# Second product of the feed-forward block, eight products of quarters against seven (Strassen's scheme, one level)

## The chip, the cores and the metric

One core of one Trainium2 chip runs the whole program. The metric is device time in microseconds (us), as the median of three runs: 895.64 us (895.19 to 899.47). One further execution was recorded by the profiler. TensorE is called PE below, VectorE DVE, ScalarE ACT, GpSimd POOL; SP and ACT issue the transfers (DMAs).

## The reference

The kernel computes one transformer block for 512 tokens of width 1024: a mixer of three attention branches, an attention over a memory, and a gated feed-forward network, each added to the residual stream, and a last normalization. Only the feed-forward part and the end bear on the change:

```python
def _swiglu(u, w_in, w_out):
    a = u @ w_in
    return (jax.nn.silu(a[..., :D_FF]) * a[..., D_FF:]) @ w_out

h = h + _swiglu(_rmsnorm(h, norm_ffn[l]), w_ffn_in[l], w_ffn_out[l])
return _rmsnorm(h, norm_final)
```

`D_FF` is 2816, that is 22 chunks of 128. The second product, `(silu * gate) @ w_out`, multiplies a 512 x 2816 matrix A by the 2816 x 1024 matrix B = `w_ffn_out`.

## The kernel before, in words

Every large product is made of three matmuls in place of one, since each operand is held as two float32r parts: `hi`, the rounded value, and `lo`, what is left. `split` (L60 to L68) makes the parts: one cast for `hi` (ACT, L58) and one subtraction for `lo` (L66, on DVE, or on POOL where `lo_eng` says so). `mm3` issues hi*hi (L94), hi*lo (L95) and lo*hi (L96). A matmul has 128 rows of the contraction and up to 512 columns.

The instructions are written in program order, and a scheduler sets the order of each engine's queue from it when the program is built; each engine then works through its own queue in order, and semaphores carry the waits between them. A tile pool with `bufs=n` hands out n buffers under a name; a tile that takes a buffer over waits until every reader of the tile before it is done.

The feed-forward's first product (`ff_pair`, called for pairs of chunks) fills four PSUM banks, applies tanh and two DVE operations (L824, L825), and splits the result into `act_hi` and `act_lo` of one chunk. Its weights come through `load_split`: 512 KB by DMA into `raw` (three buffers), then `whi` and `wlo` (three each).

The second product then runs over the 22 chunks k. It holds the whole 512 x 1024 result in eight PSUM banks, `wo` and `y` (four blocks of 128 tokens by two halves of 512 columns), and for each chunk loads 128 rows of B, splits them and issues 8 x 3 matmuls of 512 columns:

```python
mm3(yb[c, half], [t[:, cc(c)] for t in act[k]], [t[:, 0, n] for t in ws[k]], k == 0, False)
```

The last five chunks (`tail`) are done block by block, so that the end of one block of tokens (residual addition L868, squares L869, the scale of the normalization in `rms_scale`, the product with the gain L875 to L878, and the store) lies beside the matmuls of the next.

## Time and profile before

| | |
|---|---|
| median of three runs | 895.64 us |
| the profiled execution's own time | 895.49 us |
| its span in the profile | 893.7 us |
| PE busy | 857.5 us, 96% of the span |
| DVE, ACT, POOL busy | 57%, 46%, 16% |
| granted PE clock, mean | 0.994 of full speed |

How to read it: the span is the time from the first to the last recorded instruction; the run's own time is 1.79 us longer. An engine's busy time is the union of its instructions. A matmul's duration in the timeline is longer than the step from one to the next, because matmuls overlap in the array; the step is what a stream of them costs. A row such as `[2.24 <-DVE rs]` gives the engine's idle time ahead of the instruction and whom it waited for.

### The profile page before, as it was taken

How to read it: one execution, taken by the hardware profiler on the slowest of the kernel's cores; microseconds unless marked ns; L12 is line 12 of the kernel's file. 1: busy time of each engine (PE TensorE's matmuls, PEld its weight loads, DVE VectorE, ACT ScalarE, POOL GpSimd, SP SyncE). 2: the span in 40 equal slices, each digit the busy share in tenths (PEclk: the TensorE clock that was granted, in tenths of full speed). 3: DMA queues.
4: the chain of work that ended last, by engine and by line, in shares of the span. 5: the costliest groups of instructions: out<-in, count | busy, mean ns of one | idle time of the engine just before them, and what ended most of it. 6: DMA issues, size and time to landing. Idle time of an engine off the chain costs nothing.

```text
span 893.7 us, 13079 instructions
## 1 busy us (share of the span) xinstructions
PE 857.5 (96%) x5012; PEld 732.9 (82%) x5012; DVE 506.3 (57%) x1155; ACT 411.3 (46%) x779; POOL 141.0 (16%) x116
## 2 busy tenths in 40 slices
...
GB/s 321 88 110 24 37 64 120 141 49 25 58 35 27 97 94 140 187 175 249 124 149 183 182 48 166 190 165 94 95 95 95 95 98 105 124 96 95 95 19 76
DMA packets 93710, 99.00 MB, mean 111 GB/s; under 512 B 4656, under 2 KB 81616, under 8 KB 93648
## 3 DMA queue, kind: packets, MB, share of 16 engines
...
## 4 chain that ended last, share of the span: by engine, by line
PE 86%; DVE 6%; ACT 4%; DMA 2%; issue 1%; POOL 0%; SPq 0%; DVEq 0%; ACTq 0%; POOLq 0%
PE wo L95 9%; PE wo L96 9%; PE wo L94 9%; PE gf L95 6%; PE gf L94 6%; PE gf L96 6%; PE ff L96 4%; PE ff L94 4%; PE ff L95 4%; PE gm L94 3%; PE gm L95 3%; PE gm L96 3%; PE y L96 2%; PE y L95 2%; PE y L94 2%; PE av L101 2%
## 5 line engine op out<-in xcount | busy, mean ns | idle before, releaser
L58 ACT CAST whi<-raw 128x1024 fp32r<-128x1024 f32 (+1 forms) x167 | 174.6, 1048 | 283.3 <-PE y L96 70.1
L66 DVE TENSOR_TENSOR wlo<-raw,whi 128x1024 fp32r<-128x1024 f32 (+1 forms) x131 | 164.0, 1255 | 202.1 <-ACT whi L58 201.8
L66 POOL TENSOR_TENSOR wlo<-raw,whi 128x1024 fp32r<-128x1024 f32 x36 | 89.1, 2479 | 311.1 <-ACT whi L58 266.6
L95 PE MATMUL wo<-ut_lo,whi 128*128 128x256 f32 (+1 forms) x320 | 105.8, 331 | 0.0
L96 PE MATMUL wo<-ut_hi,wlo 128*128 128x256 f32 (+1 forms) x320 | 105.0, 328 | 0.0
L94 PE MATMUL wo<-ut_hi,whi 128*128 128x256 f32 (+1 forms) x320 | 104.8, 328 | 0.0
L96 PE MATMUL gf<-ut_hi,wlo 128*128 128x512 f32 (+1 forms) x192 | 69.8, 363 | 0.0
L94 PE MATMUL gf<-ut_hi,whi 128*128 128x512 f32 (+1 forms) x192 | 69.3, 361 | 0.0
L95 PE MATMUL gf<-ut_lo,whi 128*128 128x512 f32 (+1 forms) x192 | 69.3, 361 | 0.0
L94 PE MATMUL ff<-ut_hi,whi 128*128 128x512 f32 (+1 forms) x192 | 67.9, 354 | 0.0
L95 PE MATMUL ff<-ut_lo,whi 128*128 128x512 f32 (+1 forms) x192 | 67.9, 354 | 0.0
L96 PE MATMUL ff<-ut_hi,wlo 128*128 128x512 f32 (+1 forms) x192 | 67.9, 354 | 0.0
L95 PEld LDWEIGHTS wo<-ut_lo,whi 128*128 128x128 f32 x320 | 61.4, 192 | 6.3 <-issue 1.0
L94 PEld LDWEIGHTS wo<-ut_hi,whi 128*128 128x128 f32 x320 | 61.2, 191 | 5.7 <-issue 0.7
L96 PEld LDWEIGHTS wo<-ut_hi,wlo 128*128 128x128 f32 x320 | 61.3, 192 | 5.6 <-issue 0.4
L876 POOL TENSOR_TENSOR ut_hi<-ut_hi,ut_lo 128x512 f32<-128x512 f32 x4 | 5.1, 1293 | 361.9 <-ACT ut_hi L875 361.9
L94 PE MATMUL gm<-whi,ut_hi 128*128 128x256 f32 (+1 forms) x160 | 47.5, 297 | 0.0
L95 PE MATMUL gm<-wlo,ut_hi 128*128 128x256 f32 (+1 forms) x160 | 46.7, 292 | 0.0
L96 PE MATMUL gm<-whi,ut_lo 128*128 128x256 f32 (+1 forms) x160 | 46.5, 291 | 0.0
L96 PEld LDWEIGHTS gf<-ut_hi,wlo 128*128 128x128 f32 x192 | 36.2, 188 | 5.7 <-issue 1.2
L94 PEld LDWEIGHTS gf<-ut_hi,whi 128*128 128x128 f32 x192 | 36.2, 188 | 5.3 <-issue 0.8
L95 PEld LDWEIGHTS gf<-ut_lo,whi 128*128 128x128 f32 x192 | 36.2, 188 | 5.3 <-issue 0.8
...
## 6 DMA issues: line engine op xcount, KB each, us to landing
raw<-in_w_ffn_in_dram SPq DMA_DIRECT2D x56, 512.0 KB, 3.6
raw<-in_w_in_dram SPq DMA_DIRECT2D x46, 512.0 KB, 3.8
raw<-in_w_ffn_out_dram SPq DMA_DIRECT2D x22, 512.0 KB, 3.5
raw<-in_w_out_dram SPq DMA_DIRECT2D x16, 512.0 KB, 3.6
raw<-in_w_up_dram SPq DMA_DIRECT2D x8, 512.0 KB, 4.0
xt<-in_x_dram SPq DMA_DIRECT2D x4, 512.0 KB, 9.3
raw<-in_w_mem_kv_dram SPq DMA_DIRECT2D x4, 512.0 KB, 3.9
raw<-in_w_mem_q_dram SPq DMA_DIRECT2D x4, 512.0 KB, 3.9
```

Of the source, the lines that this page charges most:

```text
L58: nc.scalar.copy(dst, src)
L66: (lo_eng or nc.vector).tensor_sub(dst_lo, src, dst_hi.bitcast(F32))
L94: nc.tensor.matmul(dst, lh, rh, start=first, stop=False, skip_group_check=True)
L95: nc.tensor.matmul(dst, lh, rl, start=False, stop=False, skip_group_check=True)
L96: return nc.tensor.matmul(dst, ll, rh, start=False, stop=last, skip_group_check=True).ins
L101: nc.tensor.matmul(dst[64 * x:64 * x + 64], lhs[x], rhs[x], start=first, stop=last, skip_group_check=True)
L876: nc.gpsimd.tensor_mul(yo[:, n], yo[:, n], gain[:, n])
```

## The change

A and B are cut into quarters: A11 and A21 are the first and the last 256 tokens of chunks 0 to 10, A12 and A22 those of chunks 11 to 21; B11, B12 (chunks 0 to 10) and B21, B22 (chunks 11 to 21) are the left and right 512 columns. Seven products of quarters take the place of eight. They are those of Winograd's form of the scheme, with S1 = A21+A22, S2 = S1-A11, S3 = A11-A21, S4 = A12-S2, T1 = B12-B11, T2 = B22-T1, T3 = B22-B12, and B21-T2.

- `ff_pair` no longer splits its result. It keeps it in plain float32 (`sa` tiles for A11 and A21, `sb` tiles for A12 and A22), and `combine` forms S1, S2 and S4 on DVE and S3 on POOL, 128 x 256 each, once per chunk pair (k, k+11).
- First loop, k from 0 to 10, called a **turn** below: two DMAs bring 128 rows of B each; three DVE subtractions of 128 x 512 write T1, T3 and T2 into one tile `ts`, of which there is one buffer; ACT casts `ts` (128 x 1536), POOL subtracts for its `lo` part (128 x 1536); B11 is split on ACT and DVE; A11, S3 (one 128 x 512 piece) and S1, S2 (another) are split on ACT and DVE into `ahi` and `alo` (two buffers each); DVE writes B21-T2 over the A11/S3 tile. From turn 1 on the weights' parts lie in the buffers of the first product's input (`big`, the tiles `ut_hi` and `ut_lo`), turn k in half k%2. PE then does four products, 24 matmuls of 512 columns: A11*B11 into banks X, S2*T2 into Y, S1*T1 into Z, S3*T3 into V.
- Between the loops, ACT copies X into `u2`, DVE adds Y to it, and Z and V are added to the residual rows; six additions of 128 x 512 on POOL spread `u2` (L921 to L923).
- Then three passes of 66 matmuls each add a product into banks X, Z and V: A12*B21, S4*B22, A22*(B21-T2). A pass goes by pairs of chunks (`operands`), five pairs and one single; the `lo` part of the weights is made by DVE and POOL in turn. The second halves of `w_ffn_out` are loaded again, 12 more DMAs of 512 or 256 KB. The store of the first 256 tokens lies in the third pass, and the last three chunks of that pass are done block by block.

```diff
@@ after.py, lines 806 to 843 @@
+    def combine(k):
+        a11, a21 = (qta[k][:, x, :] for x in range(2))
+        a12, a22, s1, s2, s4 = (qtb[k][:, x, :] for x in range(5))
+        nc.vector.tensor_add(s1, a21, a22)
+        nc.vector.tensor_sub(s2, s1, a11)
+        nc.gpsimd.tensor_sub(a21, a11, a21)
+        nc.vector.tensor_sub(s4, a12, s2)
...
-            hi, lo = act[2 * fp + f]
-            split(hi[:, cols], lo[:, cols], s)
+            dst = (qtb if x else qta)[k][:, 0:2, :].rearrange("p a n -> p (a n)")
+            nc.vector.scalar_tensor_tensor(dst[:, cols], s, 0.5, b, op0=ALU.mult, op1=ALU.mult)
+            if x and cols.stop == S:
+                combine(k)
@@ after.py, lines 869 to 923 @@
+    def rows_split(src, lo_eng=nc.vector):
+        t = [f1.tile([P, 1024], F32R, name=n, bufs=2) for n in ("ahi", "alo")]
+        for (d0, n), ap in src:
+            split(t[0][:, d0:d0 + n], t[1][:, d0:d0 + n], ap, lo_eng=lo_eng)
+        return t
+    def product(banks, ka, kb, first, last):
+        for c in range(2):
+            mm3(banks[c], [t[:, cc(c)] for t in ka], kb, first, last)
+    for k in range(NH):
+        raw = []
+        for kk in (k, k + NH):
+            r = stage.tile([P, WT], F32, name="raw", bufs=3)
+            nc.sync.dma_start(r, wf[:, kk, :])
+            raw.append(r)
+        b11, b12 = raw[0][:, 0:512], raw[0][:, 512:1024]
+        b21, b22 = raw[1][:, 0:512], raw[1][:, 512:1024]
+        ts = f1.tile([P, 3, 512], F32, name="ts")
+        t1, t3, t2 = (ts[:, x, :] for x in range(3))
+        nc.vector.tensor_sub(t1, b12, b11)
+        nc.vector.tensor_sub(t3, b22, b12)
+        nc.vector.tensor_sub(t2, b22, t1)
...
+            wh, wl = (t[:, k % 2] for t in big)
+            w = [(wh[:, x, :], wl[:, x, :]) for x in range(4)]
+            split(wh[:, 1:4, :], wl[:, 1:4, :], ts, lo_eng=nc.gpsimd)
+        split(w[0][0], w[0][1], b11)
+        flat = qta[k].rearrange("p a n -> p (a n)")
+        a = rows_split([((0, 512), flat), ((512, 512), qtb[k][:, 2:4, :].rearrange("p a n -> p (a n)"))])
+        nc.vector.tensor_sub(flat, b21, t2)
+        for banks, x, y in ((X, 0, 0), (Y, 3, 3), (Z, 2, 1), (V, 1, 2)):
+            product(banks, [t[:, 256 * x:256 * x + 256] for t in a], w[y], k == 0, k == NH - 1)
...
+    for c in range(2):
+        nc.gpsimd.tensor_add(h[c][:, d1], u2[:, c, :], h[c][:, d1])
+        nc.gpsimd.tensor_add(h[2 + c][:, d0], u2[:, c, :], h[2 + c][:, d0])
+        nc.gpsimd.tensor_add(h[2 + c][:, d1], u2[:, c, :], h[2 + c][:, d1])
@@ after.py, lines 930 to 981 @@
+    def operands(k0, x, src):
+        ks = range(k0, min(k0 + 2, NH))
+        lo_eng = (nc.vector, nc.gpsimd)[k0 // 2 % 2]
...
+            hl = load_split((len(ks), 512), [wf[:, NH + k0:NH + k0 + len(ks), src]], lo_eng)
+            w = [[t[:, i, :] for t in hl] for i in range(len(ks))]
+        a = rows_split([((256 * i, 256), qtb[k][:, x, :]) for i, k in enumerate(ks)])
...
+    for banks, x, src, rows, n in ((X, 0, d0, 0, d0), (Z, 4, d1, 0, d1)):
+        for k0 in range(0, NH, 2):
+            for a, w, k in operands(k0, x, src):
+                product(banks, a, w, False, k == NH - 1)
+        for c in range(2):
+            nc.vector.tensor_add(h[rows + c][:, n], banks[c], h[rows + c][:, n])
+    for c in range(2):
+        store(c)
+    held = []
+    for k0 in range(0, NH, 2):
+        ops = operands(k0, 1, None)
...
+    for c in range(2):
+        for a, w, k in held:
+            mm3(V[c], [t[:, cc(c)] for t in a], w, False, k == NH - 1)
+        nc.vector.tensor_add(h[2 + c][:, d0], V[c], h[2 + c][:, d0])
+        store(2 + c)
```

What this makes of the queues, at three places. First, DVE at the start of the second product before, where each of 22 chunks has one subtraction (`wlo`); the rows ahead of it end the first product:

```order
L825 SCALAR_TENSOR_TENSOR sa_7946<-sa_7946,ff_7824 128x512 [waits DVE_49,PE_49]
L66 TENSOR_TENSOR act_lo20_7819<-sa_7946,act_hi20_7818 128x512 [waits Activation_49]
L825 SCALAR_TENSOR_TENSOR sa_7952<-sa_7952,ff_7825 128x512 [waits PE_49]
L66 TENSOR_TENSOR act_lo21_7821<-sa_7952,act_hi21_7820 128x512 [waits Activation_49]
L66 TENSOR_TENSOR wlo_8036<-raw_8033,whi_8035 128x1024 [waits DMAHW0_49,Activation_49]
L66 TENSOR_TENSOR wlo_8066<-raw_8063,whi_8065 128x1024 [waits DMAHW1_49,Activation_49]
```

and DVE in turn 4 now (the other turns read alike; `ut_lo` is the `lo` part of B11, `ts_8122` the one `ts` buffer of this turn, `sa4` the A11/S3 tile, L907 writes B21-T2 over it):

```order
L66 TENSOR_TENSOR ut_lo_7937<-raw_8118,ut_hi_7936 128x512 [waits DMAHW4_49,Activation_49]
L892 TENSOR_TENSOR ts_8122<-raw_8118 128x512 [waits DVE_49,Pool_49]
L893 TENSOR_TENSOR ts_8122<-raw_8120,raw_8118 128x512 [waits DMAHW5_49]
L894 TENSOR_TENSOR ts_8122<-raw_8120,ts_8122 128x512 [waits DVE_49]
L66 TENSOR_TENSOR alo_8131<-sa4_6394,ahi_8130 128x512 [waits PE_49,Activation_49]
L907 TENSOR_TENSOR sa4_6394<-raw_8120,ts_8122 128x512 [waits DVE_49]
L66 TENSOR_TENSOR alo_8131<-sb4_7492,ahi_8130 128x512 [waits Activation_49]
L66 TENSOR_TENSOR ut_lo_7937<-raw_8161,ut_hi_7936 128x512 [waits DMAHW6_49,Activation_49]
```

Seven DVE operations stand where one stood per chunk, two chunks a turn; the first write to `ts` waits for POOL.

Second, POOL's queue, which before has four multiplications left after the weights of the memory attention:

```order
L66 TENSOR_TENSOR mg_lo_4425<-gh_5447,mg_hi_4424 128x256 [waits Activation_49]
L66 TENSOR_TENSOR wlo_5900<-raw_5897,whi_5899 128x1024 [waits DMAHW3_49,Activation_49,Pool_49]
L66 TENSOR_TENSOR wlo_5922<-raw_5919,whi_5921 128x1024 [waits DMAHW4_49,Activation_49,Pool_49]
L876 TENSOR_TENSOR ut_hi_7970<-ut_hi_7970,ut_lo_7971 128x512 [waits DMAHW3_49,PE_49,Activation_49]
L876 TENSOR_TENSOR ut_hi_7970<-ut_hi_7970,ut_lo_7971 128x512 [waits Activation_49] x3
```

and now, from the last turns to the first pass (nine rows like the first stand before it; `wlo` rows belong to pairs 2, 4 and 6 of the first pass):

```order
L66 TENSOR_TENSOR ut_lo_7937<-ts_8380,ut_hi_7936 128x1536 [waits Activation_49]
L66 TENSOR_TENSOR wlo_8464<-raw_8461,whi_8463 128x1024 [waits DMAHW3_49,Activation_49]
L921 TENSOR_TENSOR h0_4412<-u2_8419,h0_4412 128x512 [waits DVE_49]
L922 TENSOR_TENSOR h2_4414<-u2_8419,h2_4414 128x512 [waits DMAHW1_49]
L921 TENSOR_TENSOR h1_4413<-u2_8419,h1_4413 128x512 [waits DVE_49]
L922 TENSOR_TENSOR h3_4415<-u2_8419,h3_4415 128x512 [waits DMAHW1_49]
L923 TENSOR_TENSOR h2_4414<-u2_8419,h2_4414 128x512 [waits DVE_49]
L923 TENSOR_TENSOR h3_4415<-u2_8419,h3_4415 128x512 [waits DVE_49]
L66 TENSOR_TENSOR wlo_8512<-raw_8509,whi_8511 128x1024 [waits DMAHW5_49,Activation_49]
L66 TENSOR_TENSOR wlo_8560<-raw_8557,whi_8559 128x512 [waits DMAHW7_49,Activation_49]
```

POOL has a 128 x 1536 subtraction in every turn, and in the first pass the six additions stand ahead of the second `wlo`.

Third, DVE in the third pass, in which the last normalization of the first 256 tokens (`rs`, L958) now stands between the parts that PE needs (`wlo`, `alo`); before, those operations stood behind the last `wlo`:

```order
L66 TENSOR_TENSOR wlo_8504<-raw_8501,whi_8503 128x1024 [waits DMAHW1_49,Activation_49]
L66 TENSOR_TENSOR wlo_8510<-raw_8507,whi_8509 128x1024 [waits DMAHW2_49,Activation_49]
L868 TENSOR_TENSOR h0_4412<-wo_7962,h0_4412 128x512 [waits PE_49]
L868 TENSOR_TENSOR h0_4412<-wo_7963,h0_4412 128x512 [waits PE_49]
L870 TENSOR_TENSOR ssf_8513<-ssf_8513 128x1 [waits Activation_49]
L115 TENSOR_SCALAR rs_8549<-ssf_8513 128x1 [waits DVE_49]
L117 TENSOR_SCALAR rs_8549<-rs_8549 128x1 [waits DVE_49]
L119 SCALAR_TENSOR_TENSOR rs_8549<-rs_8549 128x1 [waits DVE_49]
```

and now:

```order
L119 SCALAR_TENSOR_TENSOR rs_8717<-rs_8717 128x1 [waits DVE_49]
L115 TENSOR_SCALAR rs_8734<-ssf_8730 128x1 [waits DVE_49]
L120 SCALAR_TENSOR_TENSOR rs_8717<-rs_8717 128x1 [waits DVE_49]
L66 TENSOR_TENSOR alo_8778<-sb3_7483,ahi_8777 128x256 [waits Activation_49]
L958 SCALAR_TENSOR_TENSOR ut_hi_8434<-h0_4412,rs_8717,ut_lo_8435 128x512 [waits DMAHW0_49,DVE_49]
L958 SCALAR_TENSOR_TENSOR ut_hi_8434<-h0_4412,rs_8717,ut_lo_8435 128x512
L117 TENSOR_SCALAR rs_8734<-rs_8734 128x1
L66 TENSOR_TENSOR wlo_8796<-sa4_6394,whi_8795 128x512 [waits Activation_49]
L119 SCALAR_TENSOR_TENSOR rs_8734<-rs_8734 128x1 [waits DVE_49]
L66 TENSOR_TENSOR wlo_8796<-sa5_6399,whi_8795 128x512 [waits Activation_49]
L120 SCALAR_TENSOR_TENSOR rs_8734<-rs_8734 128x1 [waits DVE_49]
L66 TENSOR_TENSOR alo_8802<-sb4_7492,ahi_8801 128x256 [waits PE_49,Activation_49]
```

In the first row list PE's operands are all ready ahead of the normalization; in the second they queue behind it.

## Rows read from the trace of the kernel before

**Rows 1.** The page, parts 1 and 4: engines' busy time; the chain that ended last.

```profile
PE 857.5 (96%) x5012; PEld 732.9 (82%) x5012; DVE 506.3 (57%) x1155; ACT 411.3 (46%) x779; POOL 141.0 (16%) x116
...
PE 86%; DVE 6%; ACT 4%; DMA 2%; issue 1%; POOL 0%; SPq 0%; DVEq 0%; ACTq 0%; POOLq 0%
```

**Rows 2.** Windows: stretch, then busy us per engine, granted PE clock, DMA share, GB/s.

```profile
760.00:800.00 40.00, 40.00 (x178) 33.14 (x177) 12.19 (x13) 10.06 (x11) 0.00 (x0) 1.00 0.35 107
...
840.00:880.00 40.00, 40.00 (x178) 33.14 (x177) 13.58 (x30) 9.44 (x17) 2.54 (x2) 1.00 0.15 49
```

**Rows 3.** Timeline of PE (start, us, what): first and last matmul of the product.

```profile
765.82 0.39 PE L94 MATMUL wo<-whi,act_hi 128*128 128x512 f32 x1
...
885.28 0.39 PE L96 MATMUL y<-whi,act_lo 128*128 128x512 f32 x1
```

**Rows 4.** Groups by form, from 680 us on (busy, mean ns of one).

```profile
L66 DVE TENSOR_TENSOR wlo<-raw,whi 128x1024 fp32r<-128x1024 f32 x34 | 41.7, 1225 | 111.6 <-ACT whi L58 111.6
L58 ACT CAST whi<-raw 128x1024 fp32r<-128x1024 f32 x33 | 34.8, 1054 | 117.2 <-PE y L96 70.1 <-issue 18.7 <-PE wo L95 14.8
...
L66 DVE TENSOR_TENSOR act_lo<-sa,act_hi 128x512 fp32r<-128x512 f32 x9 | 6.2, 690 | 3.4 <-ACT act_hi L58 3.4
L58 ACT CAST act_hi<-sa 128x512 fp32r<-128x512 f32 x9 | 5.6, 619 | 10.6 <-DVE sa L825 10.6
```

**Rows 5.** Timeline of POOL: operations with two inputs, three sizes, none overlapping such on DVE.

```profile
303.78 1.29 POOL L404 TENSOR_TENSOR g<-g 128x512 f32<-128x512 f32 x1 [10.02 <-DVE g L388]
...
325.72 2.40 POOL L66 TENSOR_TENSOR wlo<-raw,whi 128x1024 fp32r<-128x1024 f32 x1 [3.20 <-ACT whi L58]
...
390.54 0.74 POOL L66 TENSOR_TENSOR mg_lo<-g,mg_hi 128x256 fp32r<-128x256 f32 x1 [16.24 <-ACT mg_hi L58]
```

**Rows 6.** Timeline of DVE and POOL at 360 us: operands of both in SBUF.

```profile
360.43 1.22 DVE L66 TENSOR_TENSOR wlo<-raw,whi 128x1024 fp32r<-128x1024 f32 x1
361.56 2.36 DVE L120 SCALAR_TENSOR_TENSOR rs<-rs 128x1 f32<-128x1 f32 x1
...
364.21 0.16 DVE L120 SCALAR_TENSOR_TENSOR rs<-rs 128x1 f32<-128x1 f32 x1
...
360.51 3.39 POOL L66 TENSOR_TENSOR wlo<-raw,whi 128x1024 fp32r<-128x1024 f32 x1 [2.49 <-ACT whi L58]
```

**Rows 7.** Timeline of DVE and POOL at 514 us: wo is a PSUM bank.

```profile
518.19 0.41 DVE L825 SCALAR_TENSOR_TENSOR sa<-sa,wo 128x256 f32<-128x256 f32 x1
...
513.96 4.73 POOL L66 TENSOR_TENSOR wlo<-raw,whi 128x1024 fp32r<-128x1024 f32 x2 [31.45 <-DMA raw<-in_w_ffn_in_dram]
```

**Rows 8.** DMA issues: KB each, median us from issue to landing.

```profile
raw<-in_w_ffn_out_dram SPq DMA_DIRECT2D x22, 512.0 KB, 3.5
```

**Rows 9.** Timeline of the last row block: POOL, then DVE.

```profile
883.17 2.54 POOL L876 TENSOR_TENSOR ut_hi<-ut_hi,ut_lo 128x512 f32<-128x512 f32 x2 [4.26 <-ACT ut_hi L875]
...
885.70 0.69 DVE L868 TENSOR_TENSOR h<-y,h 128x512 f32<-128x512 f32 x1 [2.71 <-PE y L96]
...
889.10 1.41 DVE L878 SCALAR_TENSOR_TENSOR ut_hi<-h,rs,ut_lo 128x512 f32<-128x512 f32 x2
```

**Rows 10.** Timeline of PE around 465 us: an idle stretch and what follows.

```profile
465.49 1.73 PE L133 MATMUL ps<-cst,u 128*128 128x128 f32 x8 [2.24 <-DVE rs L115]
...
467.23 0.41 PE L96 MATMUL wo<-ut_hi,wlo 128*128 128x256 f32 x1
467.44 0.41 PE L94 MATMUL wo<-ut_hi,whi 128*128 128x256 f32 x1
...
470.01 0.28 PE L94 MATMUL wo<-ut_hi,whi 128*128 128x256 f32 x1
470.13 0.28 PE L95 MATMUL wo<-ut_lo,whi 128*128 128x256 f32 x1
```

**Rows 11.** Windows of the same stretch.

```profile
466.00:467.00 1.00, 1.00 (x7) 1.00 (x5) 1.00 (x1) 0.59 (x1) 0.00 (x0) 0.50 0.59 225
...
469.00:470.00 1.00, 1.00 (x9) 1.00 (x9) 0.31 (x2) 0.62 (x1) 0.00 (x0) 0.90 0.82 328
```

More of the change, by code (lines that the diff above doesn't have):

```diff
@@ L844, in block_kernel, with bank_pair @@
     y_ps = ctx.enter_context(tc.tile_pool(name="y_ps", bufs=4, space=PSUM))
-    yb = {(c, half): (wo_ps.tile([P, 512], F32, name="wo") if c < 2 else y_ps.tile([P, 512], F32, name="y"))
-          for c in range(NT) for half in range(2)}
+    def bank_pair(first):
+        return [(wo_ps.tile([P, 512], F32, name="wo") if first else y_ps.tile([P, 512], F32, name="y")) for c in range(2)]
+    X, Y, Z, V = bank_pair(True), bank_pair(True), bank_pair(False), bank_pair(False)
     wf = col_view(A["w_ffn_out"][0], 0, D)
-    y_out, gain = (utp.tile([P, NK, S], F32, name=n).rearrange("p a b -> p (a b)") for n in ("ut_hi", "ut_lo"))
@@ new lines, in block_kernel @@
+    for k in range(NH):
[11 more added lines that the diff above has]
+        nc.vector.tensor_sub(t2, b22, t1)
+        if k == 0:
+            wh, wl = ([stage.tile([P, WT], F32R, name=n, bufs=3).rearrange("p (a n) -> p a n", a=2) for _ in range(2)] for n in ("whi", "wlo"))
+            w = [(wh[x // 2][:, x % 2, :], wl[x // 2][:, x % 2, :]) for x in range(4)]
+            for x in range(3):
+                split(w[x + 1][0], w[x + 1][1], ts[:, x, :], lo_eng=nc.gpsimd if x else None)
+        else:
+            wh, wl = (t[:, k % 2] for t in big)
[7 more added lines that the diff above has]
+            product(banks, [t[:, 256 * x:256 * x + 256] for t in a], w[y], k == 0, k == NH - 1)
```

59 lines of the change are left out of this document (34 added, 25 removed).

## Prediction

> **What bounds the kernel now.** I read the page's busy times and the chain of waits first: PE is busy 96% of the span and carries 86% of the chain [rows 1], so only what PE issues, or waits for, counts. Then the windows of the second product: PE is busy for all of every 40 us, at the full clock, while DVE is busy for a third of it or less and POOL nearly idle [rows 2]. Then the timeline: the product's first matmul starts at 765.82, the last at 885.28 [rows 3]. Between them lie 528 matmuls (22 chunks x 8 x 3), so the step is 119.46/527 = 0.2267 us and there is no hole. The end, from the last matmul's start to 893.7, takes 8.4 us. The reader is to see that the stage is PE's alone, and that what feeds it has much room.
>
> **What goes.** Eight products become seven: 11 x 24 = 264 matmuls in the turns and 3 x 66 = 198 in the passes, 462 in all. 66 x 0.2267 = **15.0 us less** of PE. Everything else in the change is the price of feeding PE.
>
> **What a turn now needs.** On DVE seven operations of 128 x 512 (three for T1, T3, T2, one for B21-T2, three `lo` parts): 0.69 each alone [rows 4], about 0.65 back to back since neighbours overlap a little, as the 1.41 for two in [rows 9] leaves room for. On ACT a cast of 128 x 1536: 0.619 for 512 and 1.054 for 1024 columns [rows 4] give 1.49 by the same slope, and 0.62 for each of three more. On POOL a subtraction of 128 x 1536: 0.74, 1.29 and 2.40 for 256, 512 and 1024 columns [rows 5] give 3.51. PE's 24 matmuls take 5.44. No engine alone exceeds that. Two things do.
>
> First, the chain through the single `ts` buffer. The order rows show that DVE may write T1 of the next turn only when POOL is done with this one. So T1, T3, T2, ACT's cast and POOL's subtraction follow each other turn after turn: 2.0 + 1.49 + 3.51 + 0.1 for handovers (an allowance) = 7.1.
>
> Second, DVE and POOL exclude each other. At 360.43 DVE subtracts with both inputs in SBUF; POOL's subtraction beside it takes 3.39 in place of 2.40, longer by about what DVE still had to do; the next DVE operation, on 128 x 1 elements, takes 2.36 where its like takes 0.16, and ends with POOL's [rows 6]. A DVE operation with one input in PSUM is not held up: 0.41 amid POOL's work [rows 7]. All seven DVE operations of a turn have both inputs in SBUF. Their sum with POOL's is 7 x 0.62 + 3.51 = 7.85 at the least.
>
> Together: the `lo` part of S1, S2 waits for an ACT cast that stands behind the cast of `ts`, so POOL gets in first. After POOL's end DVE must do that part, B11's, T1, T3 and T2: 5 x 0.65 = 3.2, then 1.49 and 3.51 follow, with 0.1: **8.3 us a turn**. Where a row speaks of up to 1024 columns only, the 1536 are an extension by slope.
>
> The Trainium skill, "SBUF — State Buffer", section "Who interferes with whom", says that the pair of ports is held for the whole instruction; up to 1024 columns [rows 6] agree, and no row shows 1536. By that rule the turn is 8.3; were a long instruction to let go in between, it would be nearer 7.1.
>
> **The turns summed**, from the start of PE's first matmul as zero. Turn 0 is prepared during the first product (its parts lie in `whi` and `wlo`), so PE has 5.4 us of work. Turn 1's cast needs the first product's input gone, and DVE and POOL still work on the last chunks' combinations: POOL ends turn 1 at about 6.0. Turn 2 adds the rest of the combinations (about 1.5 us of DVE, 0.74 of POOL) ahead of T1, and turns 2 and 3 have both A parts behind POOL's hold: ends at 15.8 and 25.1. Seven turns of 8.3 bring POOL to 83. PE then has the last turn's matmuls and must wait for `u2`: that copy stands on ACT behind the cast of the third weight pair, whose DMA (3.5 us [rows 8]) waits for a `raw` buffer that the last B21-T2 frees. That is 7.2 us after POOL's end, or 9.3 if POOL's next `wlo` (2.40) gets in between; I take 8.3. The passes start at 91.5 where 11 x 5.44 = 59.8 would be without a wait: **31.7 more**, bounds 27 (turn of 7.85) and 35.
>
> **The first pass** (PE 15.0). DVE and POOL in turn: two `wlo` of 1.22, the remaining `alo` parts of 256 at 0.41 (3.7), POOL's 2.40, 2.40 and 1.29, and the six additions of 1.29 [rows 4, 5, 7]: 20.0. If the pair ahead is done before the pass starts, 2.4 less. 2.6 to 5.0 too much; I take **4**, since the additions stand ahead of the second `wlo`. **The second pass**: 3.7 + 4.5 + 6.1 = 14.3, just covered; **0.5**. **The third**: six `wlo` halves 4.1, eleven `alo` 4.5, four gain products 2.8, some 18 tiny two-input operations 3.4, POOL's five halves 6.5: 21.3 against 15.0, of which about 1.3 can be done ahead: **5**, bounds 2 and 7. Here the normalization of the first 256 tokens, behind the matmuls before, stands in front of PE's operands.
>
> **The end.** The last block's chain is as before (DVE at 885.70, gain products from 889.10 [rows 9]). But POOL's two multiplications of the block before, done by 885.7 then, now fall among the nine tiny operations, and each can hold them for 1.27: 0 to 2.5, I take **2**.
>
> The DMAs (1 MB per 8.3 us, each landing 3.5 us after its issue [rows 8]) arrive with 2 us to spare in a turn, since the `raw` buffer is free after T3. The combinations during the first product, two or four DVE operations a pair for two casts and two subtractions saved, lie beside PE's full stretch [rows 2]: nothing; without that cover they would be under 2 us a pair. The changed scheduling before 560 us: nothing, give or take 1.
>
> **The sum**: -15.0 + 31.7 + 4 + 0.5 + 5 + 2 = +28.2, on the profiled execution's 895.49: **923.7 us**. The median shown is 0.15 above that execution, which changes nothing.
>
> **Rivals.**
> First, PE stays the bound (faster). It holds if a turn comes under 5.44: POOL's subtraction would have to take under 1.9, or T1 not wait for it. For: every engine's own sum is under 5.44. Against: three sizes on POOL lie on one line [rows 5], and the wait is in the order rows. -15.0 and some 2 us of the hand-over between loops: 882.5. 5%.
> Second, the chain alone counts and the exclusion hardly bites: turns of 7.1, the passes start at 74 + 1, and DVE's own length costs 3 in the passes: -15.0 + 15 + 3 = +3, **899**. Against: [rows 6]. 7%.
> Third, the slow clock. After PE was idle for 2.24 us, the granted clock was 0.50, that is 1.2 GHz, from 466 until it rose during the window of 469 [rows 10, 11], and the step of 256 columns was 0.21 in place of 0.12 [rows 10]. In each turn PE idles about 2.8. Some 3.2 us at that clock cost 3.2 x (1 - 0.12/0.21) = 1.4 us of work, which vanishes in the turn's own wait (5.44 + 1.4 < 8.3); that is why the sum has nothing for it. If the clock stayed low through the turns, 24 matmuls would take 5.44 x 0.21/0.12 = 9.5 and PE would set the turn: 9 x 1.2 more, **935**. Against: the rows show the rise after 3 us of work, and a turn has five. 7%. [...]
>
> **Numbers.** The forecast has 81%; the rest as above. Its own bounds: -15 + 27 + 2.6 + 0 + 2 + 0 = +17 and -15 + 35 + 5 + 1.5 + 7 + 2.5 = +36, so 912 to 931; 908 to 932 leaves some room below for a lighter exclusion. A measurement here tells 0.5% (4.5 us) from no change. Slower by more: 81 + 7 and a little of the second rival, 0.89; within: 0.06; faster: 0.05.
>
> **What would show it.** Right: 66 PE instructions fewer; in the turns PE busy about two thirds of the time, idle for DVE and POOL; POOL's ten 1536-column rows 3.5 or longer; DVE's 512-column rows with a mean well over 0.69; T1 released by POOL; a turn of about 8.3. Wrong: turns under 6, or DVE rows at 0.69 beside a busy POOL.

## The result, and the profile after

The changed kernel takes 920.12 us (median; 918.98 to 922.42), the kernel before, on the same chip, 896.32: slower by 2.64% (ratio 1.0264, 95% interval 1.0245 to 1.0283). The forecast was 923.7 with a range of 908 to 932. The profiled execution took 918.98 us with a span of 917.1, 23.4 more than before.

The page, parts 1 and 4, as in [rows 1]:

```profile
PE 857.0 (93%) x4946; PEld 723.8 (79%) x4946; DVE 601.4 (66%) x1267; ACT 436.8 (48%) x831; POOL 217.1 (24%) x154
...
PE 74%; DVE 13%; ACT 5%; issue 4%; DMA 2%; POOL 1%; SPq 0%; DVEq 0%; ACTq 0%; POOLq 0%
...
L66 POOL TENSOR_TENSOR ut_lo<-ts,ut_hi 128x1536 fp32r<-128x1536 f32 x10 | 34.8, 3483 | 42.6 <-ACT ut_hi L58 42.5
```

PE has 66 instructions fewer (5012 to 4946), and its share of the chain fell from 86% to 74%; DVE's rose from 6% to 13%. PE's busy time hardly fell, although 15 us of matmuls are gone: a part of what is left ran at the low clock (the mean granted clock is 0.981, before 0.994). The windows, as in [rows 2] (stretch, busy us of PE, its weight loads, DVE, ACT and POOL, granted PE clock, DMA share, GB/s):

```profile
760.00:800.00 40.00, 34.01 (x136) 25.94 (x135) 34.05 (x38) 13.99 (x19) 18.62 (x8) 0.96 0.34 106
800.00:840.00 40.00, 32.79 (x119) 24.01 (x119) 35.76 (x35) 15.82 (x20) 17.39 (x5) 0.91 0.43 132
840.00:880.00 40.00, 35.58 (x140) 27.28 (x139) 35.35 (x39) 20.14 (x36) 23.03 (x12) 0.91 0.45 145
```

Where PE was busy for all of 40 us and DVE for 10 to 14, PE is now busy for 33 to 36 and DVE for 34 to 36. Some 14 of DVE's 35.76 are waiting inside its instructions: in each of the five turns there, one operation takes 3.52 to 3.58 where its like takes 0.68. One steady turn shows it. The timeline of DVE, POOL and ACT in the turn that starts with POOL's subtraction at 802.59:

```profile
803.07 3.52 DVE L66 TENSOR_TENSOR alo<-sb,ahi 128x512 fp32r<-128x512 f32 x1 [0.82 <-ACT ahi L58]
806.51 0.68 DVE L66 TENSOR_TENSOR ut_lo<-raw,ut_hi 128x512 fp32r<-128x512 f32 x1
807.12 0.68 DVE L892 TENSOR_TENSOR ts<-raw 128x512 f32<-128x512 f32 x1
807.72 0.68 DVE L893 TENSOR_TENSOR ts<-raw 128x512 f32<-128x512 f32 x1
808.32 0.68 DVE L894 TENSOR_TENSOR ts<-raw,ts 128x512 f32<-128x512 f32 x1
...
802.59 3.46 POOL L66 TENSOR_TENSOR ut_lo<-ts,ut_hi 128x1536 fp32r<-128x1536 f32 x1 [4.62 <-ACT ut_hi L58]
810.67 3.50 POOL L66 TENSOR_TENSOR ut_lo<-ts,ut_hi 128x1536 fp32r<-128x1536 f32 x1 [4.62 <-ACT ut_hi L58]
...
809.11 1.48 ACT L58 CAST ut_hi<-ts 128x1536 fp32r<-128x1536 f32 x1 [5.04 <-DVE ts L894]
```

The reader should follow it as a circle. POOL ends at 806.05. The DVE subtraction that had started at 803.07, and takes 0.68 elsewhere, ends 0.54 later. Then B11's `lo` part, T1, T3 and T2 follow at steps of 0.60; T2 ends at 809.00; ACT casts until 810.59; POOL starts again at 810.67. That is 8.08 us. From 786.38 to 843.09 seven such circles take 56.71, or 8.10 each.

The product's places on PE, as in [rows 3]: first matmul, first of each pass, and last.

```profile
765.59 0.39 PE L94 MATMUL wo<-whi,ahi 128*128 128x512 f32 x1
...
856.10 0.39 PE L94 MATMUL wo<-whi,ahi 128*128 128x512 f32 x1
...
871.59 0.39 PE L94 MATMUL y<-whi,ahi 128*128 128x512 f32 x1
...
886.89 0.39 PE L94 MATMUL y<-whi,ahi 128*128 128x512 f32 x1
...
906.63 0.39 PE L96 MATMUL y<-whi,alo 128*128 128x512 f32 x1
```

Against 59.85 for 264 matmuls and 14.96 for 66 at a step of 0.2267, these give the terms of the sum:

| term, us | predicted | measured |
|---|---|---|
| 66 matmuls fewer | -15.0 | -15.0 |
| passes start, from the product's first matmul | 91.5, +31.7 | 90.51, +30.7 |
| first pass, over 15.0 | +4 | 15.49, +0.5 |
| second pass | +0.5 | 15.30, +0.3 |
| third pass (906.63 + 0.23 - 886.89) | +5 | 19.97, +5.0 |
| end (917.1 - 906.63, against 8.42) | +2 | 10.47, +2.0 |
| product's start (765.59 against 765.82) | 0 | -0.2 |
| sum | +28.2 | +23.4 |

### The profile page after: what moved, and what is told of

Its sections match the earlier page's. It is cut to its first block, busy times and chain, and to the rows that moved or that the text cites. A ratio compares the mean times of both kernels' runs of the same rounds, so it can differ in the third digit from the quotient of the medians.

```text
span 917.1 us, 13240 instructions
## 1 busy us (share of the span) xinstructions
PE 857.0 (93%) x4946; PEld 723.8 (79%) x4946; DVE 601.4 (66%) x1267; ACT 436.8 (48%) x831; POOL 217.1 (24%) x154
## 4 chain that ended last, share of the span: by engine, by line
PE 74%; DVE 13%; ACT 5%; issue 4%; DMA 2%; POOL 1%; SPq 0%; DVEq 0%; ACTq 0%; POOLq 0%
PE wo L96 7%; PE wo L95 7%; PE wo L94 7%; PE gf L94 5%; PE gf L95 5%; PE gf L96 5%; PE ff L94 4%; PE ff L95 4%; PE ff L96 4%; PE gm L94 3%; PE gm L95 3%; PE gm L96 3%; DVE alo L66 3%; PE av L101 2%; PE ps L565 1%
## 5 line engine op out<-in xcount | busy, mean ns | idle before, releaser
L58 ACT CAST whi<-raw 128x1024 fp32r<-128x1024 f32 (+1 forms) x158 | 164.0, 1040 | 233.4 <-PE wo L95 73.2
L66 DVE TENSOR_TENSOR wlo<-raw,whi 128x1024 fp32r<-128x1024 f32 (+2 forms) x116 | 145.3, 1254 | 125.4 <-ACT whi L58 125.3
L66 POOL TENSOR_TENSOR wlo<-raw,whi 128x1024 fp32r<-128x1024 f32 (+1 forms) x42 | 101.9, 2432 | 323.0 <-ACT whi L58 278.3
L812 POOL TENSOR_TENSOR sa<-sa 128x256 f32<-128x256 f32 x11 | 13.5, 1228 | 221.7 <-DVE sb L810 221.7
L66 DVE TENSOR_TENSOR alo<-sb,ahi 128x256 fp32r<-128x256 f32 (+1 forms) x44 | 51.6, 1199 | 12.6 <-ACT ahi L58 10.9
L66 POOL TENSOR_TENSOR ut_lo<-ts,ut_hi 128x1536 fp32r<-128x1536 f32 x10 | 34.8, 3483 | 42.6 <-ACT ut_hi L58 42.5
```

The lines of the kernel that those rows point to most:

```text
L58: nc.scalar.copy(dst, src)
L66: (lo_eng or nc.vector).tensor_sub(dst_lo, src, dst_hi.bitcast(F32))
L812: nc.gpsimd.tensor_sub(a21, a11, a21)
```

## The experiments

Theory A is the prediction's: DVE's operations, all with both inputs in SBUF, and POOL's exclude each other, and this together with the order of the queue makes the turn. Theory B is its second rival: the chain through the one `ts` buffer makes the turn alone. Where an expectation below gives the letters to theories of its own, it says so. The measured ratios are against the kernel before.

### POOL busy, but reading nothing

```diff
-            split(wh[:, 1:4, :], wl[:, 1:4, :], ts, lo_eng=nc.gpsimd)
+            copy(nc.scalar, wh[:, 1:4, :], ts)
+            lo = wl[:, 1:4, :].rearrange("p a n -> p (a n)")
+            for x in range(2):
+                nc.gpsimd.tensor_sub(lo[:, 0:1], ts[:, 0, 0:1], wh[:, 1, 0:1].bitcast(F32))
+                if x == 0:
+                    nc.gpsimd.memset(lo.bitcast(F32), 0.0)
+                    nc.gpsimd.memset(lo.bitcast(F32), 0.0)
```

> One ts buffer, and POOL is still busy between ACT's cast and the release of ts, but reads next to nothing: its subtraction of 128 x 1536 is replaced by two memsets of the lo tile, with a subtraction of one column ahead of them (which waits for the cast) and one behind them (which releases ts). The lo part of T1, T3, T2 is left out (zero in all but one column). P is POOL's time for the four; no run shows a memset of that size, so it is read from this one. Theory A (DVE's operations with both inputs in SBUF are held only by what POOL reads): DVE rows of 512 columns stay at 0.68 beside the memsets and the turn is the chain alone, 1.8 + 0.1 + 1.49 + 0.1 + P, or PE's 5.44 if that is more; with P near 3.5 it is 7.0 and the time 909. Theory B (POOL's work as such holds DVE, or its length sets the turn): DVE rows of about P, a turn of 8.1 or P + 4.6, 920 with P near 3.5.

Measured: 904.12 us (ratio 1.0090, 1.0075 to 1.0104). One turn, POOL above, DVE below:

```profile
802.39 0.19 POOL L906 TENSOR_TENSOR ut_lo<-ts,ut_hi 128x1 fp32r<-128x1 f32 x1 [3.60 <-ACT ut_hi L58]
802.64 1.38 POOL L908 MEMSET ut_lo<- 128x1536 f32 x1
804.08 1.38 POOL L909 MEMSET ut_lo<- 128x1536 f32 x1
805.54 0.19 POOL L906 TENSOR_TENSOR ut_lo<-ts,ut_hi 128x1 fp32r<-128x1 f32 x1
...
802.86 0.69 DVE L66 TENSOR_TENSOR alo<-sa,ahi 128x512 fp32r<-128x512 f32 x1 [0.94 <-ACT ahi L58]
803.47 0.68 DVE L66 TENSOR_TENSOR alo<-sb,ahi 128x512 fp32r<-128x512 f32 x1
805.77 0.69 DVE L892 TENSOR_TENSOR ts<-raw 128x512 f32<-128x512 f32 x1 [1.61 <-POOL ut_lo L906]
```

POOL is occupied from 802.39 to 805.73, P = 3.34, nearly as long as with its subtraction. The DVE operations beside the memsets take 0.69 and 0.68, where the change shows 3.52. T1 still waits for POOL, so the chain is there, and the turn (798.82 to 805.77, T1 to T1) is 6.95: 1.8 + 0.1 + 1.49 + 0.1 + 3.34 = 6.83 and a little. This is the turn as the chain alone would make it, and the change is 1.15 us a turn slower than it, of which 0.14 is the shorter P. The expectation's own second theory, that POOL's work as such holds DVE or that its length sets the turn, falls with the 0.69 and the 6.95. Theory A holds; the time is 5 below the 909 expected, since P was under 3.5 and the first turns were spared too (POOL ends turns 2 and 3 at steps of 6.9, in the change 9.4 and 9.3). The Trainium skill, "SBUF — State Buffer", section "Who interferes with whom", says that a DVE instruction with two SBUF inputs contends with a GpSimd instruction that reads SBUF and not with one that only writes it; the 0.69 beside memsets and the 3.52 beside a subtraction agree.

### The `lo` part of `ts` on DVE, with one and with two `ts` buffers

```diff
-            split(wh[:, 1:4, :], wl[:, 1:4, :], ts, lo_eng=nc.gpsimd)
+            split(wh[:, 1:4, :], wl[:, 1:4, :], ts)
```

> One ts buffer as in the change, but the lo part of ts (128 x 1536) is made by DVE and no longer by POOL: the chain stays, POOL has nothing to do in the turns. DVE's operation extends to 1.75 us by the slope of 0.69 for 512 and 1.22 for 1024 columns. Theory A (exclusion sets the turn): DVE's own sum of 7 x 0.60 + 1.75 = 5.95 takes the place of 8.1, ten turns 21 us less: 899 (895 to 903). Theory B (chain alone): 1.8 + 0.1 + 1.49 + 0.1 + 1.75 = 5.25 is under PE's 5.44, 895 or a little below. A third theory, that the turn is set by PE's low clock after each wait or by the arrival of the 1 MB: little is gained, 912 or more.

> Both edits: lo of ts on DVE and two ts buffers. Theory A: DVE is the bound at 5.95 a turn whether or not the chain is there, so the time is that of the kernel with the one edit on DVE within 2 us, 898 (895 to 902). If the chain still cost something after the move to DVE, this is faster than that kernel by over 3 us.

Measured: 900.48 us with one buffer (1.0048, 1.0029 to 1.0066), 898.64 with `bufs=2` for `ts` besides (1.0024, 1.0010 to 1.0038). DVE with one buffer, two turns apart by 5.99:

```profile
796.52 1.76 DVE L66 TENSOR_TENSOR ut_lo<-ts,ut_hi 128x1536 fp32r<-128x1536 f32 x1
...
802.51 1.76 DVE L66 TENSOR_TENSOR ut_lo<-ts,ut_hi 128x1536 fp32r<-128x1536 f32 x1
```

Taking work from POOL and giving it to DVE, the busier engine, made a turn 2.1 us shorter: 1.76 on DVE replaces 3.48 on POOL, for most of which DVE stood still. The third theory falls: neither the DMA nor the clock set the turn. With two buffers DVE runs ahead, and six of PE's turns (2 to 7) go at 5.44; the passes start 62.8 after the first matmul, only 3 more than PE needs.

But the first pass, 15.49 in the change, now takes 20.65 (829.30 to 849.95). DVE, POOL and PE there, in the kernel with two buffers:

```profile
835.19 7.54 DVE L66 TENSOR_TENSOR alo<-sb,ahi 128x256 fp32r<-128x256 f32 x6
...
836.35 2.90 POOL L923 TENSOR_TENSOR h<-u,h 128x512 f32<-128x512 f32 x2
839.21 2.57 POOL L66 TENSOR_TENSOR wlo<-raw,whi 128x1024 fp32r<-128x1024 f32 x1
...
836.73 0.50 PE L96 MATMUL wo<-whi,alo 128*128 128x512 f32 x1 [1.97 <-DVE alo L66]
```

Six operations of 128 x 256 take 7.54, where one takes 0.41, since POOL's additions and its `wlo` hold them. This is the "first pass +4" of the prediction, a little larger. In the change six such operations take 7.43 (from 856.93), but PE waits only 0.23 for them.

### Two `ts` buffers alone, and a buffer more for B

```diff
-        ts = f1.tile([P, 3, 512], F32, name="ts")
+        ts = f1.tile([P, 3, 512], F32, name="ts", bufs=2)
```

> Two ts buffers in place of one: T1 of the next turn no longer waits for POOL's subtraction of this one; every operation stays. Theory A (DVE and POOL exclude each other): what is left of a turn is the sum of seven DVE operations at their step of 0.60 and POOL's 3.48, 7.7 us in place of the 8.10 of the steady turns, so some 3 us less in all: 917 (914 to 920). Theory B (the chain through the one ts buffer alone set the turn): with the chain gone nothing on DVE (4.2) or POOL (3.5) exceeds PE's 5.44, the turns fall to PE's, some 25 us less: 895.

Measured: 926.15 us (1.0344, 1.0321 to 1.0366), slower than the change by 6. Theory B is refuted again, but A's 917 is missed as well. The timeline of DVE and POOL, one turn:

```profile
813.10 3.81 DVE L892 TENSOR_TENSOR ts<-raw 128x512 f32<-128x512 f32 x1 [1.27 <-DMA raw<-in_w_ffn_out_dram]
...
812.90 3.46 POOL L66 TENSOR_TENSOR ut_lo<-ts,ut_hi 128x1536 fp32r<-128x1536 f32 x1 [5.36 <-ACT ut_hi L58]
821.70 3.50 POOL L66 TENSOR_TENSOR ut_lo<-ts,ut_hi 128x1536 fp32r<-128x1536 f32 x1 [5.34 <-ACT ut_hi L58]
```

T1 of the next turn is now the operation that POOL holds, and two `alo` parts and B21-T2 follow it ahead of T3 and T2: six operations end between POOL's end and ACT's cast, where the change has five, and T1 had waited 1.27 for a DMA. Which of the two made the turn longer? The next kernel takes the wait for the DMA away:

```diff
-            r = stage.tile([P, WT], F32, name="raw", bufs=3)
+            r = stage.tile([P, WT], F32, name="raw", bufs=3) if kk < NH else f1.tile([P, WT], F32, name="rawb")
...
-    u2 = f1.tile([P, 2, 512], F32, name="u2")
+    u2 = f1.tile([P, 3, 512], F32, name="ts", bufs=2)
```

> The kernel with two ts buffers (8.83 a turn, 926) had T1 wait 1.3 for the DMA of raw in each turn, since three raw buffers serve two halves a turn. Here the lower half of B has a buffer of its own (rawb), the upper half keeps the three; u2 takes a buffer of ts. Theory: the DMA wait was the extra length; T1 then runs in the gap while ACT casts, five DVE operations of 0.60, 1.6 and 3.5 remain, 8.1 a turn, and the time is the change's own or a little below, 919 (915 to 921). Were the order of DVE's queue as such to blame (T1 caught behind POOL's subtraction), the turn would stay at 8.8 and the time at 926.

Measured: 922.07 us (1.0293, 1.0277 to 1.0309), and DVE and POOL show:

```profile
813.52 3.18 DVE L66 TENSOR_TENSOR alo<-sa,ahi 128x512 fp32r<-128x512 f32 x1 [1.77 <-ACT ahi L58]
...
817.23 0.68 DVE L892 TENSOR_TENSOR ts<-raw 128x512 f32<-128x512 f32 x1
...
812.68 3.48 POOL L66 TENSOR_TENSOR ut_lo<-ts,ut_hi 128x1536 fp32r<-128x1536 f32 x1 [5.21 <-ACT ut_hi L58]
821.37 3.44 POOL L66 TENSOR_TENSOR ut_lo<-ts,ut_hi 128x1536 fp32r<-128x1536 f32 x1 [5.21 <-ACT ut_hi L58]
```

No wait for a DMA is left, and the turn is still 8.69: T1 stands in the queue behind an `alo` that POOL holds, the third of again six operations that end between POOL's end and the cast. The expectation that T1 would use the gap under the cast was wrong. With n operations between POOL's end and the cast, a turn is about n x 0.60 + 0.1 + 1.49 + 0.1 + 3.46: 8.15 for five (measured 8.10) and 8.75 for six (8.69 here; 8.80, with the DMA wait, above). A second buffer lifts the wait, but only the order of DVE's queue could use it. (The 4 us between these two kernels lie mostly behind the turns: the passes start 2.9 after POOL's last subtraction here, 7.8 there.)

### ACT's cast and POOL's subtraction in three pieces

```diff
-            split(wh[:, 1:4, :], wl[:, 1:4, :], ts, lo_eng=nc.gpsimd)
+            for x in range(3):
+                split(w[x + 1][0], w[x + 1][1], ts[:, x, :], lo_eng=nc.gpsimd)
```

> One ts buffer, POOL keeps the lo part, but ACT's cast and POOL's subtraction of 128 x 1536 go in three pieces of 128 x 512, so that T1's pieces start while DVE is still at T3 and T2. Chain: T1 0.6 + 0.1 + cast 0.62 + 0.1 + three POOL pieces of 1.25 = 5.2, under PE's 5.44. Theory A (exclusion: DVE gets only the gaps between pieces): 7 x 0.60 + 3 x 1.25 = 7.95 a turn, about what it was, 918 (914 to 921), and DVE operations held for up to 1.3 where they were held for 2.9. Theory B (chain alone): the turns fall to PE's 5.44 or near it, 896 (894 to 900).

Measured: 913.78 us (1.0208, 1.0163 to 1.0253; the four runs lie between 910.78 and 919.72, and the interval touches the change's, so the turns say more than the time), turns of 7.52 (POOL's first pieces at 799.12 and 806.64). DVE, then POOL:

```profile
799.46 1.78 DVE L66 TENSOR_TENSOR ut_lo<-raw,ut_hi 128x512 fp32r<-128x512 f32 x1
801.17 1.78 DVE L66 TENSOR_TENSOR alo<-sa,ahi 128x512 fp32r<-128x512 f32 x1
...
799.12 4.97 POOL L66 TENSOR_TENSOR ut_lo<-ts,ut_hi 128x512 fp32r<-128x512 f32 x3 [2.54 <-ACT ut_hi L58]
```

A DVE operation is held for one piece and then goes through before the next: two of them lie within POOL's 4.97 (3 x 1.25 + 2 x 0.60 = 4.95). So the hold is by instruction, not by stretch. The turn is far from Theory B's 5.44, but 0.43 below the sum of 7.95 that was expected of Theory A. The rows show where that lies: from the three operations beside the pieces to the next one it is 1.71, 1.82 and 1.58, that is 1.11, 1.22 and 0.98 above the step of 0.60, 3.31 in sum, where three pieces of 1.25 had been put at 3.75.

### The passes

```diff
-        lo_eng = (nc.vector, nc.gpsimd)[k0 // 2 % 2]
+        lo_eng = (nc.vector, nc.gpsimd)[k0 // 2 % 2 if src is not None else 0]
```

> The change with one edit: the lo parts of the weights of the third pass are all made by DVE, none by POOL; the normalization of the first 256 tokens keeps its place. Theory A (POOL's halves hold DVE, that is what makes the third pass 5.0 longer than its 15.0): DVE's own sum is eleven wlo of 0.62, eleven alo of 0.40, 2.8 and 3.4 less what is done ahead, 16.5, and the pass takes 16.7 as it did with POOL out of everything: 3.2 less, 916.9 (916 to 918). Theory B (the normalization's place alone sets it): the wait of 2.6 stays, 919 or more.

Measured: 916.02 us (1.0235, 1.0212 to 1.0258). The third pass takes 16.88 (890.59 to 907.47) in place of 19.97. Theory A holds in the main: POOL's halves cost 3.1 of the 5.0, directly or by the low clock behind PE's longer wait (see the third pass in the next section), and 1.9 are left to the normalization's place and DVE's own sum. (The profiled execution was the longest of its four, 919.5 against 914.8 to 916.4, with a second pass of 18.5; the other kernels show 15.0 to 15.8 there. In its trace ACT waits 2.17 for a transfer to `raw` until 873.57, and PE then 1.63 for POOL's `wlo` and 0.99 for DVE's `alo`; why the transfer came late is open.)

I also tried to move the normalization of the first 256 tokens behind the third pass:

```diff
-    for c in range(2):
-        store(c)
...
-        store(2 + c)
+    for c in range(4):
+        store(c)
```

> The normalization and store of the first 256 tokens are moved from the third pass to behind the last matmul; all else as in the change. Theory A (the 18 tiny operations and four gain products stand in front of PE's operands): the wait of 2.6 in the third pass is gone, the pass takes 15.3 in place of 20.0, and the end grows by two more normalizations of 1.9 + 1.3 on DVE, 6.4: 922 (919 to 925). Theory B (the third pass is short of lo parts anyway, since POOL's halves hold DVE): a wait of over 1 us stays in the pass, which takes 17 or more, 924 or above.

Measured: 918.87 us (1.0255, 1.0241 to 1.0269), no difference from the change that can be told. The edit did not do what it says: the scheduler put the normalizations back among the operands of the third pass, which took 19.54. So it tells nothing of either theory.

The six additions of `u2` went to DVE in another kernel (`nc.gpsimd` to `nc.vector` in L921 to L923):

> The change with one edit: the six additions of u2 between the loops on DVE (6 x 0.60) in place of POOL (6 x 1.29, or 7.7). Theory A (in the change the first pass was fed by two pairs that were ready when it began, so that POOL's additions cost it next to nothing): the first pass stays within 1 us of its 15.5, 919 to 921. Theory B (the additions do hold up the first pass, and something else hid it): the pass or what follows is shorter by over 2 us, 918 or less; or, if DVE has no 3.6 us to spare there, longer by as much, 922 or more.

Measured: 920.37 us (1.0284, 1.0267 to 1.0301). The time is Theory A's, but not by its reason: the first pass grew to 18.72 and the passes began 88.6 after the first matmul, not 90.5. The start of 88.6 is no work of the additions, since two other kernels with the same turns have it as well (88.5 and 88.6). In those two the first pass takes 16.4 and 16.5, so the additions on DVE made it 2.2 to 2.3 longer: DVE had no 3.6 us to spare there. That freeing POOL gave the rest back is likely but not shown.

### POOL out of the turns and the passes

```diff
-        ts = f1.tile([P, 3, 512], F32, name="ts")
+        ts = f1.tile([P, 3, 512], F32, name="ts", bufs=2)
...
-            split(wh[:, 1:4, :], wl[:, 1:4, :], ts, lo_eng=nc.gpsimd)
+            split(wh[:, 1:4, :], wl[:, 1:4, :], ts)
...
-        lo_eng = (nc.vector, nc.gpsimd)[k0 // 2 % 2]
+        lo_eng = nc.vector
...
+        if n == d0:
+            for c in range(2):
+                nc.vector.tensor_add(h[c][:, d1], u2[:, c, :], h[c][:, d1])
+                nc.vector.tensor_add(h[2 + c][:, d0], u2[:, c, :], h[2 + c][:, d0])
+                nc.vector.tensor_add(h[2 + c][:, d1], u2[:, c, :], h[2 + c][:, d1])
```

> From the kernel with lo of ts on DVE and two ts buffers (898.6): the lo parts of all three passes on DVE as well, and the six additions of u2 on DVE, behind the first pass. POOL is left with the two multiplications of the end. If exclusion is what the passes lose, DVE needs 3.7 + 6.4 in the first, 13.8 in the second and 16.5 in the third against PE's 15.0: sum on 895.5 of -15.0 (PE), +0.7 (start, as that kernel showed), +3.0 (turns, as there), +0.5, +0.5, +1.5 to 2.5 (passes), +1 (end): 888 (885 to 892), faster than the kernel before. If the passes lose for another reason (DMA, ACT, the normalization's place), 895 to 899.

Measured: 888.93 us (0.9920, 0.9907 to 0.9932), faster than the kernel before by 0.8%. The windows, as in [rows 2]:

```profile
780.00:800.00 20.00, 20.00 (x90) 16.57 (x89) 19.77 (x27) 12.02 (x16) 0.00 (x0) 1.00 0.57 182
800.00:820.00 20.00, 19.70 (x85) 15.40 (x84) 20.00 (x29) 9.82 (x13) 0.00 (x0) 1.00 0.51 163
```

PE and DVE are both full, at the full clock, and POOL has nothing to do. The passes start 63.0 after the first matmul and take 16.0, 15.0 and 16.7.

Two more edits on it. First the gain product of the third block of tokens on DVE too:

```diff
-            if c == 2:
-                nc.scalar.activation(yo[:, n], h[c][:, n], AF.Copy, scale=y)
-                nc.gpsimd.tensor_mul(yo[:, n], yo[:, n], gain[:, n])
-            else:
-                nc.vector.scalar_tensor_tensor(yo[:, n], h[c][:, n], y, gain[:, n], op0=ALU.mult, op1=ALU.mult)
+            nc.vector.scalar_tensor_tensor(yo[:, n], h[c][:, n], y, gain[:, n], op0=ALU.mult, op1=ALU.mult)
```

> From the kernel without POOL in the turns and the passes (888.9): the gain product of the third block of tokens goes to DVE as well, so that POOL does nothing after the first product. Theory: the two tiny operations of the last block that POOL held for 1.24 and 1.19 take 0.22 and 0.16 again, 2.0 less, and two gain products of 0.7 are added on DVE: the end, 10.9 from the last matmul's start, shortens by 0.7 (0 to 2), 888.2. If the held rows were no part of the chain that ends last, the time is the same or up to 1.3 more.

Measured: 888.14 us (0.9911, 0.9895 to 0.9927). The end, from the last matmul's start, is 9.6 (885.6 - 875.98) in place of 10.9 (886.3 - 875.41), and the two held rows are gone; the difference of the medians is as expected but within the intervals. This is the fastest version that ran, 0.9% under the kernel before.

Then S1 and S2 of the first five pairs of chunks split during the first product:

```diff
+        if k < 5:
+            sc = f1.tile([P, 2, half_s], F32, name="sc")
+            s1, s2 = sc[:, 0, :], sc[:, 1, :]
...
+        if k < 5:
+            hl[k] = [f1.tile([P, 512], F32R, name=f"{n}{k}") for n in ("sh", "sl")]
+            split(hl[k][0], hl[k][1], sc.rearrange("p a n -> p (a n)"))
```

> From the kernel with the gain product on DVE: S1 and S2 of the first five pairs of chunks are split already during the first product, where DVE has room, so that turns 0 to 4 have one DVE operation of 0.60 and one cast on ACT less; the others as before; u2 takes a buffer of ts. Theory (DVE's sum of 5.9 sets the later turns, which begin late since DVE has used up its lead): 3.0 us of DVE less, the passes start 60.5 to 61 after the first matmul in place of 63.0, 2 to 2.5 us less in all: 886. If the first product has no room for the ten more operations on DVE, PE waits there and nothing is won.

Measured: 889.68 us (0.9922, 0.9905 to 0.9938): nothing won. The first product kept its pace (it ended at 765.4 as before), but the passes start 63.5 after the first matmul, not 60.5. The room DVE gained in the first turns did not help the later ones; what keeps it from getting further ahead (two `ts`, three `raw`, two halves of `ut_hi`) was not tried.

## Why the prediction was right, and where not

**What goes**: right, 66 instructions and 15.0 us.

**What a turn needs**: right. 8.10 for 8.3, and by the steps given: POOL 3.48 for 3.51, ACT 1.48 for 1.49, five operations between POOL's end and the cast, at 0.60 rather than 0.65. The extension by slope from 1024 to 1536 columns [rows 5] held, and so did the reading of [rows 6]: held for the whole of 128 x 1536. The experiment with memsets shows the cause, not only the sum.

**The turns summed**: POOL ends turn 1 at 5.5 (767.58 + 3.55 - 765.59; predicted 6.0), turn 2 at 15.0 (15.8), the last at 81.0 (83). The step from there to the passes, taken at 8.3 between bounds of 7.2 and 9.3, was 9.6, and it went by another path than the prediction's, in which PE waits for `u2`. Rows of POOL, DVE, ACT and PE, and a window:

```profile
843.09 3.45 POOL L66 TENSOR_TENSOR ut_lo<-ts,ut_hi 128x1536 fp32r<-128x1536 f32 x1 [4.62 <-ACT ut_hi L58]
846.49 2.84 POOL L66 TENSOR_TENSOR wlo<-raw,whi 128x1024 fp32r<-128x1024 f32 x1
...
847.01 2.87 DVE L66 TENSOR_TENSOR alo<-sb,ahi 128x512 fp32r<-128x512 f32 x1
...
851.08 1.22 DVE L66 TENSOR_TENSOR wlo<-raw,whi 128x1024 fp32r<-128x1024 f32 x1
...
848.14 1.07 ACT L914 COPY u<-wo 128x512 f32<-128x512 f32 x2
...
849.93 0.79 PE L96 MATMUL wo<-ut_hi,alo 128*128 128x512 f32 x1 [0.78 <-DVE alo L66]
...
855.86 0.40 PE L96 MATMUL y<-ut_hi,alo 128*128 128x512 f32 x1
...
851.00:853.00 2.00, 2.00 (x6) 1.60 (x5) 2.00 (x4) 0.00 (x0) 0.03 (x1) 0.50 0.65 151
```

ACT's copy for `u2` was done at 849.21, and the passes' first matmul at 856.10 follows the last turn's last one at 855.86 without a wait. So PE did not wait for `u2`; the last turn itself came last. POOL's next `wlo` did get in between, as the upper bound supposes, but what it held was DVE's `lo` part of S1, S2 for that turn (847.01 to 849.88). PE waited for it until 849.93, 3.4 after POOL's last subtraction. The 16 matmuls then left would take 3.6 at the step of 0.2267 and took 6.2, since the granted clock was 0.50 (1.2 GHz) for most of them: 3.4 + 3.6 + 2.5 is the 9.6 but for rounding. Two kernels that are the change up to there (the first two of "The passes") show the same without most of the 2.5: POOL ends at 80.9 and 81.0, the 16 matmuls take 4.3 and 4.2, and the passes start at 88.6 and 88.5. So the prediction's reason for having nothing for the slow clock, that the turn's own wait takes it up, failed at the last turn, which has no such wait behind it. That the start of the passes came within 1.0 of the forecast is in part luck: the turns were 2 us shorter and this step 1.3 longer.

**The first pass**: the term that was mis-sized, +4 predicted and +0.5 measured. It set 20.0 of DVE's and POOL's work against PE's 15.0, but much of that was done before the pass's first matmul at 856.10. The second pair's `wlo` (POOL, 846.49) and the third pair's (DVE, 851.08) were ready, as the first pair's was, and POOL had been at its six additions since 852.97. By the prediction's own figures that is 2.40, 1.22 and 3.1 of the 20.0 (an estimate); the 13.3 left are less than 15.0. The prediction named a part of this case ("2.4 less") and did not take it, though it is the same event as the 9.3 in the step before. Taken together, both terms were +35.7 and measured +31.2. How much is done ahead hangs on how late PE comes: in the two kernels whose passes start at 88.6 and 88.5, the additions had been going for only 1.3 and 1.1 by then, and the pass takes 16.4 and 16.5. In the kernel with two buffers and `lo` on DVE, where PE starts the pass while POOL is still at the second pair's `wlo`, it takes 20.65; without POOL 16.0.

**The second and third pass, the end**: the sizes are right (+0.3, +5.0, +2.0), but the third pass's 5.0 is made up in another way. The third pass's wait and the held operations at the end, PE, then DVE, then POOL:

```profile
895.77 0.57 PE L95 MATMUL y<-wlo,ahi 128*128 128x512 f32 x1 [2.60 <-DVE wlo L66]
...
909.78 1.24 DVE L119 SCALAR_TENSOR_TENSOR rs<-rs 128x1 f32<-128x1 f32 x1
911.06 1.19 DVE L120 SCALAR_TENSOR_TENSOR rs<-rs 128x1 f32<-128x1 f32 x1
...
909.74 2.49 POOL L956 TENSOR_TENSOR ut_hi<-ut_hi,ut_lo 128x512 f32<-128x512 f32 x2 [7.08 <-ACT ut_hi L955]
```

Operations of 0.22 and 0.16 take 1.24 and 1.19, 2.05 more, the term's size. In the third pass PE waits 2.60 for a `wlo` that DVE made behind the normalization and beside POOL's halves, as predicted. But behind that wait nine matmuls, from 895.77 to 899.56, take 3.79 in place of 2.04, at a granted clock of 0.51 from 896 to 898 and 0.63 from 898 to 900. So 1.75 of the 5.0 is the low clock, for which the term had nothing; that its size fits is luck in part. The prediction also laid the pass to the normalization's place ahead of PE's operands. With POOL's halves gone and the normalization in its place the pass is 16.9, 3.1 shorter: PE's longest wait there is 1.19, and the clock behind it stays at 1.00.

**The rivals**: the first (PE stays the bound) fell with the turns of 8.10. The second (chain alone) was built with the memsets: 904 where it was put at 899, and the change is 16 above. The third (slow clock through the turns) fell: PE idles in every turn, but the clock is low in part of some turns only. PE at the start of two turns in a row, and the windows after each wait:

```profile
806.10 0.50 PE L95 MATMUL wo<-ut_lo,ahi 128*128 128x512 f32 x1 [2.00 <-POOL ut_lo L66]
...
814.22 0.50 PE L95 MATMUL wo<-ut_lo,ahi 128*128 128x512 f32 x1 [0.43 <-POOL ut_lo L66]
...
808.00:810.00 2.00, 2.00 (x6) 1.61 (x5) 1.97 (x4) 0.89 (x1) 0.00 (x0) 0.50 0.35 51
...
814.00:816.00 2.00, 1.73 (x6) 1.23 (x7) 2.00 (x4) 0.00 (x0) 0.17 (x1) 1.00 0.01 2
```

Behind the wait of 2.00 the granted clock goes to 0.50 (1.2 GHz), and the turn's matmuls end late; so the next wait is only 0.43, after which the clock stays at 1.00 (2.4 GHz). The two turns' starts lie 9.7 (802.35 to 812.03) and 6.5 (812.03 to 818.53) apart, 16.2 together, twice 8.1: the low clock used time that PE would have waited anyway, as the prediction said. Not every such wait has the low clock behind it: after the one of 2.03 that ends at 822.31 the clock stayed at 1.00, and the next, at 830.39, was 2.03 again. And where no later wait took it up, in the last turn (2.5) and in the third pass (1.75), the low clock did cost time, some 4.3 us that the sum had put at nothing. The Trainium skill, "TensorE: Matmul & The Clock Gate", section "Loop structure matters more than you think", gives as its bad case a loop with a long DMA wait between every matmul; no run here shows such a loop. In this one, where the waits of the steady turns are of 0.4 to 2.0 us in 24 matmuls, the mean clock from 800 to 840 was 0.91, and the time 920, not the rival's 935.
